# Interleaving the first two heads of differential attention with band attention, with outputs through DRAM and loads half a head ahead

## The chip, the core and the metric

The kernel runs on one core of a Trainium2 chip. The metric is the device time of one launch in microseconds (us). The core's engines are TensorE (PE in the profile; PEld is its weight load), VectorE (DVE), ScalarE (ACT) and GpSimd (POOL); SyncE (SP) issues nearly all DMA transfers of the stage that is changed.

## The reference, cut to what matters

One layer with 1024 rows of 1024 floats: a first feed-forward half step, two token mixers side by side, an output projection, a second feed-forward half step. The change touches the two mixers, A (band attention, 8 heads of 64) and B (differential attention, 4 heads, each with two score maps and values of 128).

```python
x = x + 0.5 * swiglu_ffn(rms_norm(x, ffn1_norm), ffn1_w_in, ffn1_w_out)
q_a, k_a, v_a, q_b, k_b, v_b, gate_logits = split(rms_norm(x, mix_norm) @ w_mix_in)
y_a = chunked_band_attention(q_a, k_a, v_a, rel_bias_a)         # own chunk of 64 and 8 before it
attn = softmax(s1 + bias) - lam * softmax(s2 + bias)            # B: chunk-causal, two maps
y_b = rms_norm(attn @ v_b, subln_g) * (1 - lambda_init)
g_a, g_b = split(sigmoid(gate_logits + b_gate))
x = x + (g_a * (y_a @ w_branch_a) + g_b * (y_b @ w_branch_b)) @ w_o
x = x + 0.5 * swiglu_ffn(rms_norm(x, ffn2_norm), ffn2_w_in, ffn2_w_out)
```

## The kernel before

**Stages.** The first feed-forward stage and the mixer's input projection come first; the projection writes queries, keys, values and gates to DRAM (`q_d`, `k_d`, `v_d`, `g_d`). The attention stage (pool `ps2`, from L747 on) reads them back head by head. The stage behind it (pool `ps3`) multiplies the outputs of B by `w_branch_b`, merges both branches and projects with `w_o`; the second feed-forward stage ends the kernel.

**Numbers as pairs.** A float that goes through a matmul as one operand is kept as a high and a low part (`split`, L94: a copy to the high part and a subtraction for the low part), so most products take two or three matmuls. The parts of queries share one tile `qs`, those of keys are two tiles `ks` and `kl`.

**Loads of a head.** `load_qkv` (L754 to L764) issues seven transfers on SP: `qs`, `ks`, `kl` in two halves of 512 KB each, and the values `vt` with 1024 KB. `bias_rows` (L794 to L803) fills the bias tile `nb`: two pieces of memory set by GpSimd and, for a pair of A heads, 8 transfers of 72 KB; for two B heads 4 of 128 KB and 4 of 120 KB. In A one load serves a pair of heads, so there are four loads, a0 to a3; B has four, b0 to b3, and one bias tile for two of them.

**Jobs.** A job is a Python generator whose pieces are laid out by `run` (L807): each new job is started, then each of the up to four jobs before it advances by one piece. In `jobs_a` (L815 to L874) a pair of heads is 8 jobs, each of two query blocks of 128 rows for one head: scores (L775, L776), softmax (L783, L785), scaling on GpSimd (L844), transposes (L791), the product with the values (L860), and at every second job the split of the sum into the output tile `y`. In `jobs_b` (L893 to L957) a head is 8 jobs, job i with one query block against i+1 key blocks, so the first is small and the last eight times as wide: two score maps, softmax, the difference, transposes, the product with the values (L939, L940), the norm, and a last matmul `try` (L954) that scales and transposes into `y`. All 32 jobs of A stand ahead of the 32 of B.

**The filler.** `branch_a` (L877 to L890) multiplies A's outputs with `w_branch_a` in 16 steps of 12 matmuls (tile `pb`), multiplies each result with its gate `gl`, which is loaded from DRAM in the step, and stores it as `ta`. In B, every second job calls one step (the sum `due`).

**Where a load comes in the order.** The first job of a head calls `load_qkv`, then takes an output tile, then the bias rows. All these tiles (`qs`, `ks`, `kl`, `vt`, `nb`, `y`, 8 KB in each of the 128 partitions) come from one pool of 14 buffers, `big` (L69). The outputs of all eight loads, `ys[0]` to `ys[7]`, keep their buffers until the filler and the next stage have used them, so fewer buffers are left for loads as the stage goes on.

**SP's queue.** SP issues its transfers in order. The build gives them eight semaphores in turn, so a transfer also waits until the eighth before it has landed. Temporary tiles of 2 KB (`gl`, sums, high parts) come from a pool `f` of 10 buffers. The order of instructions on each engine is fixed when the kernel is built.

Of the kernel before, what the change touches and what calls it, by code (L numbers as in the profile page):

```python
# [9 lines left out]
F32 = mybir.dt.float32  # L10
F32R = mybir.dt.float32r
# [5 lines left out]
P = 128  # L17
S = 1024
D = 1024
NT = S // P  # L20
# [24 lines left out]
RAW, WU, TF, TT = 10, 10, 10, 3  # L45
WA = 640
EA = 768
WB = 1024
HEADS = 5
SKEW = 32  # L50
EB = 1152
# [3 lines left out]
def hybrid_layer_kernel(ctx, tc, x, ffn1_norm, ffn1_w_in, ffn1_w_out, mix_norm, w_mix_in,  # L55
# [3 lines left out]
    nc = tc.nc  # L59
# [5 lines left out]
    sb = ctx.enter_context(tc.tile_pool(name="sb", bufs=1))  # L65
# [3 lines left out]
    def big(shape, name, dtype=F32R):  # L69
        return sb.tile(shape, dtype, tag="big", bufs=14, name=name)  # L70
# [51 lines left out]
    def move(eng, dst, src):  # L122

        eng.dma_start(out=dst.bitcast(F32), in_=src.bitcast(F32))
# [394 lines left out]
    def drams(n, shape, name, dtype=F32):  # L519
        return [dram.tile(shape, dtype, name=f"{name}{i}") for i in range(n)]  # L520
# [51 lines left out]
    ta_d = drams(KT, [P, S], "ta")  # L572
    diag_a = dram.tile([A_HEADS, SKEW, EA], F32, name="diag_a")
# [172 lines left out]
    ys = []  # L746
    with tc.tile_pool(name="ps2", bufs=1, space=PSUM) as ps:  # L747
# [59 lines left out]
        def run(jobs, filler=None):  # L807
            live = []
            for step, job in enumerate(list(jobs) + [None] * 4):
                for g in [job] + live[::-1] if job else live[::-1]:  # L810
                    next(g, None)
                live = (live + [job] if job else live)[-4:]


        def jobs_a(pr):  # L815
            ctx_ = {}

            def job(sb_, h):
                if not ctx_:
                    ctx_["qkv"] = load_qkv(pr)  # L820
                    ctx_["y"] = big([P, 2, S], "y")
                    ys.append(ctx_["y"])
                    ctx_["nb"] = big([P, 2, S], "nb", F32)
                    for hh in range(2):
                        bias_rows(ctx_["nb"][:, hh, :WA], diag_a, 2 * pr + hh, EA, WA)
                qkv, y, nb = (ctx_[n] for n in ("qkv", "y", "nb"))
# [44 lines left out]
                if h == 1:  # L871
                    c = slice(sb_ * 256, (sb_ + 1) * 256)
                    split(ysum, y[:, 0, c], y[:, 1, c], on_pool=True)
            return [job(sb_, h) for sb_ in range(4) for h in range(2)]  # L874


# [16 lines left out]
        def jobs_b(hb, filler):  # L893
            ctx_ = {}

            def job(i):
                if not ctx_:
                    ctx_["qkv"] = load_qkv(4 + hb)
                    ctx_["y"] = big([P, 2, S], "y")
                    ys.append(ctx_["y"])  # L900
                    if hb % 2 == 0:
                        nbs.append(big([P, 2, S], "nb", F32))
                        for hh in range(2):
                            bias_rows(nbs[-1][:, hh, :], diag_b, hb + hh, EB, WB)
                    ctx_["nb"] = nbs[-1][:, hb % 2, :]
                qkv, y, nb = (ctx_[n] for n in ("qkv", "y", "nb"))
# [45 lines left out]
                yield  # L952
                tr = ps.tile([P, 4, P], F32, tag="pt", bufs=2, name="try")
                nc.tensor.matmul(tr[:, 0, :], o1, dg, start=True, stop=True)  # L954
                c = slice(i * P, (i + 1) * P)
                split(tr[:, 0, :], y[:, 0, c], y[:, 1, c], scale=gsub)
            return [job(i) for i in range(NT)]  # L957

        jobs, nbs = [], []
        for pr in range(4):  # L960
            jobs += jobs_a(pr)
        filler = branch_a()
        due = [0]
        for hb in range(4):
            jobs += jobs_b(hb, filler)
        run(jobs)
        for _ in filler:
            pass
# [93 lines left out]
```

## Time and profile before

| what | value |
|---|---|
| time, median of 3 runs | 2185.04 us (2180.58 to 2188.15) |
| time of the profiled execution | 2184.25 us |
| its span in the profile | 2181.9 us |
| TensorE busy, share of the span | 2084.9 us, 96% |
| VectorE, ScalarE, GpSimd busy | 67%, 45%, 9% |
| bytes moved | 325.16 MB, 149 GB/s in the mean |
| granted TensorE clock, mean | 0.985 |
| attention stage | about 1076 to 1378 us of the span |

The profile is of one execution; its span leaves out 2.35 us of the measured time. A row of a windows view gives, for a stretch of the span, its length, then for each engine its busy time and number of instructions, the TensorE clock that was granted (1.00 is full speed), the busy share of the DMA engines and the rate. In a waits view a row names an instruction, what released it, the total of the time that its engine was idle ahead of it, how often, and the longest. In a timeline, the brackets at the end of a row hold the idle time just before it and its releaser.

### The profile page before, as it was taken

What the parts mean: (1) busy time and instruction counts of PE and PEld (TensorE: products, weight loads), DVE (VectorE), ACT (ScalarE), POOL (GpSimd) and SP (SyncE); (2) the same over time, 40 slices, a digit from 0 to 9 for tenths busy, and PEclk for the clock granted to TensorE, in tenths of its full rate; (3) what the DMA queues carried; (4) which work ended last, traced back from release to release, by engine and by line L of the source; (5) the groups of instructions that cost most, each with busy time, mean ns of one, the idle gap of its engine ahead of it and who ended that gap; (6) DMA issues with size and microseconds to landing.
All of it is one profiled execution on the core that took longest, in us unless ns stands there. A gap on an engine that the chain in (4) does not pass through costs nothing.

```text
span 2181.9 us, 29018 instructions
## 1 busy us (share of the span) xinstructions
PE 2084.9 (96%) x10025; PEld 1739.5 (80%) x10025; DVE 1461.3 (67%) x2678; ACT 977.4 (45%) x1911; POOL 195.6 (9%) x290
## 2 busy tenths in 40 slices
PE   6999999999999999999999878898999999999997
PEld 5788888888888788998788767676778888888886
DVE  7666565576578656556588767677766665658566
ACT  5433333334456444444588555235533333334444
POOL 2120000000000000000175233201000000000001
PEclk9999999999999999999999988999999999999999
DMA  6653233293354544443895675714543333366334
GB/s 191 175 167 113 91 107 102 91 373 105 116 167 128 164 136 164 135 151 125 210 210 122 156 180 157 243 64 145 173 130 120 96 114 97 116 221 233 98 116 158
DMA packets 273347, 325.16 MB, mean 149 GB/s; under 512 B 15292, under 2 KB 167884, under 8 KB 273200
## 3 DMA queue, kind: packets, MB, share of 16 engines
q1 hardware_dynamic: 271872, 319.55, 47.9%
q0 software_dynamic: 1184, 3.24, 0.6%
q8 instruction: 79, 1.29, 0.3%
q14 instruction: 68, 0.56, 0.1%
q10 hardware_dynamic: 144, 0.52, 0.1%
HBM read 226.45 MB, written 96.80 MB: 148 GB/s over the span
## 4 chain that ended last, share of the span: by engine, by line
PE 81%; DVE 7%; DMA 6%; ACT 3%; issue 2%; SPq 1%; POOL 0%; ACTq 0%; DVEq 0%; POOLq 0%
PE prod L128 18%; PE prod L129 18%; PE prod L130 18%; PE po L129 6%; PE po L130 6%; PE po L128 6%; DMA kl<-k 2%; DVE wlo L102 2%; PE tr L205 1%; ACT whi L97 1%; PE pt L791 1%; PE pb L128 1%; PE sc L775 1%; DMA ha<-hS 1%; PE pb L129 1%
## 5 line engine op out<-in xcount | busy, mean ns | idle before, releaser
L129 PE MATMUL po<-wlo,whi 128*128 128x512 f32 x728 | 284.7, 391 | 5.7 <-DVE wlo L102 5.5
L130 PE MATMUL po<-whi,wlo 128*128 128x512 f32 x728 | 283.4, 389 | 0.0
L97 ACT CAST whi<-raw 128x512 fp32r<-128x512 f32 x200 | 124.4, 622 | 308.6 <-PE prod L129 246.9
L97 ACT CAST whi<-T 128x512 fp32r<-128x512 f32 x196 | 121.9, 622 | 250.3 <-PE prod L129 225.1
L97 ACT CAST whi<-B 128x512 fp32r<-128x512 f32 x178 | 110.8, 623 | 266.0 <-PE po L129 258.0
L113 DVE TENSOR_TENSOR c<-prod,c 128x512 f32<-128x512 f32 x190 | 131.1, 690 | 134.6 <-PE prod L130 122.9
L102 DVE TENSOR_TENSOR wlo<-raw,whi 128x512 fp32r<-128x512 f32 x200 | 138.6, 693 | 105.1 <-ACT whi L97 66.4
L102 DVE TENSOR_TENSOR wlo<-B,whi 128x512 fp32r<-128x512 f32 x178 | 122.6, 689 | 126.7 <-ACT whi L97 126.6
L128 PE MATMUL po<-whi 128*128 128x512 f32 x728 | 198.4, 390 | 0.5 <-DVE xc L507 0.5
L102 DVE TENSOR_TENSOR wlo<-T,whi 128x512 fp32r<-128x512 f32 x196 | 134.7, 688 | 92.3 <-ACT whi L97 91.1
L139 POOL TENSOR_TENSOR r<-v,neg_half 128x1 f32<-128x1 f32 x64 | 53.8, 844 | 1326.8 <-DVE v L180 1227.1
L129 PEld LDWEIGHTS po<-wlo,whi 128*128 128x128 f32 x728 | 136.6, 188 | 37.7 <-DVE wlo L102 9.9
L128 PEld LDWEIGHTS po<-whi 128*128 128x128 f32 x728 | 136.2, 188 | 30.3 <-ACT whi L97 1.1
L130 PEld LDWEIGHTS po<-whi,wlo 128*128 128x128 f32 x728 | 136.7, 188 | 28.1
L102 DVE TENSOR_TENSOR wlo<-N,whi 128x512 fp32r<-128x512 f32 x64 | 44.1, 690 | 114.0 <-PE prod L129 62.8
L102 DVE TENSOR_TENSOR wlo<-ha,whi 128x512 fp32r<-128x512 f32 x154 | 105.7, 686 | 9.0 <-ACT whi L97 9.0
L272 ACT COPY c<-prod 128x512 f32<-128x512 f32 x186 | 103.1, 587 | 11.5 <-DMA hA<-c 4.0
L785 ACT ACTIVATE pm<-pm,mn 128x640 f32<-128x640 f32 (+7 forms) x128 | 94.1, 737 | 20.1 <-DVE mn L783 11.1
L783 DVE CUSTOM_DVE_ANT_0 pm<-sc,nb 128x640 f32<-128x640 f32 (+7 forms) x128 | 88.4, 699 | 21.5 <-PE sc L776 20.3
L97 ACT CAST whi<-ha 128x512 fp32r<-128x512 f32 x154 | 94.8, 615 | 16.9 <-PE prod L129 11.4
L128 PE MATMUL prod<-A11h,whi 128*128 128x512 f32 x240 | 96.0, 400 | 1.9 <-ACT A11h L97 1.9
L128 PE MATMUL prod<-S1h,whi 128*128 128x512 f32 x240 | 94.5, 394 | 2.4 <-ACT S1h L97 1.4
(246 smaller groups left out, 5398.3 us busy)
## 6 DMA issues: line engine op xcount, KB each, us to landing
raw<-in_ffn_w_in_dram SPq DMA_DIRECT2D x98, 512.0 KB, 4.4
raw<-in_w_mix_in_dram SPq DMA_DIRECT2D x47, 512.0 KB, 4.4
ha<-hS SPq DMA_DIRECT2D x88, 256.0 KB, 2.7
hA<-c SPq DMA_DIRECT2D x66, 256.0 KB, 4.3
ha<-hA SPq DMA_DIRECT2D x66, 256.0 KB, 2.7
B<-in_ffn_w_out_dram SPq DMA_DIRECT2D x12, 1024.0 KB, 10.6
hS<-hs SPq DMA_DIRECT2D x44, 256.0 KB, 2.8
hS<-c SPq DMA_DIRECT2D x44, 256.0 KB, 4.5
```

Of the source, the lines that this page charges most:

```text
L97: nc.scalar.copy(out=hi, in_=src)
L102: (nc.gpsimd if on_pool else nc.vector).tensor_tensor(out=lo, in0=src, in1=h, op=ALU.subtract)
L113: nc.vector.tensor_tensor(out=out_, in0=a, in1=b, op=op)
L128: nc.tensor.matmul(ps, a[0], b[0], start=first, stop=False, skip_group_check=shared)
L129: nc.tensor.matmul(ps, a[0], b[1], start=False, stop=False, skip_group_check=shared)
L130: nc.tensor.matmul(ps, a[1], b[0], start=False, stop=last, skip_group_check=shared)
L139: nc.gpsimd.tensor_tensor(out=r, in0=v, in1=neg_half, op=ALU.pow)
L205: nc.tensor.transpose(tr[:, k, :], rows[:, k * P:(k + 1) * P], ident)
L272: nc.scalar.copy(out=self.held[name], in_=p)
L775: nc.tensor.matmul(sc[:, m, :wc], qs[:, h, c], ks[:, h, kc], start=True, stop=False)
L783: nc.vector.tensor_tensor_reduce(out=d3, in0=sc, in1=nb.rearrange("p (n w) -> p n w", n=n), scale=1.0, scalar=3e38, op0=ALU.add, op1=ALU.m ...
L785: nc.scalar.activation(out=dst, in_=dst, func=AF.Exp, bias=mn, scale=-1.0, accum_out=rs)
```

## The change

- **Order of jobs.** The 16 jobs of b0 and b1 are put between the 32 jobs of A by the table `MIX` (a0.0 is job 0 of a0): b0.0 after the third A job, then one about every 2.7 A jobs; b1.0 comes after the 24th, and b1.3 to b1.7 behind the last. b2 and b3 follow as before.
- **Loads.** A head's loads are taken out of its first job into `begin()`, which now issues the bias rows ahead of `qs`, `ks`, `kl`, `vt`. The lists call `begin` early: a0 and b0 at the start, a1 before a0's fifth job, b1 before a1's first, a2 before a1's fifth, a3 before a2's fifth, b2 before a3's third, b3 after two jobs of b2.
- **Outputs.** An output is no longer kept in a `big` buffer: it is split into a small tile of pool `f` (`ya`, `yb`) and stored to `y_d` in DRAM: 16 stores of 256 KB for A, 24 of 128 KB for b0, b1 and b2. `load_y` reads them back, 1 MB each: `y0` to `y3` ahead of b2's first job, `y4` to `y6` ahead of b3's seventh. b3 writes its output tile directly.
- **Filler.** It is called only in b2 and b3, and there by every job: 16 steps in 16 jobs.
- **Pieces.** A job of B has one more `yield` ahead of `try`, and `run` keeps five jobs alive in place of four.

```diff
+MIX = [n * 12 // 32 for n in range(32)] + [16]
...
+    y_d = drams(7, [P, 2, S], "y", F32R)
...
+            for job in list(jobs) + [None] * 5:
+                if callable(job):
+                    job()
+                    continue
                 for g in [job] + live[::-1] if job else live[::-1]:
                     next(g, None)
-                live = (live + [job] if job else live)[-4:]
+                live = (live + [job] if job else live)[-5:]
...
+            def begin():
+                ctx_["nb"] = big([P, 2, S], "nb", F32)
+                for hh in range(2):
+                    bias_rows(ctx_["nb"][:, hh, :WA], diag_a, 2 * pr + hh, EA, WA)
+                ctx_["qkv"] = load_qkv(pr)
...
+                    y = sb.tile([P, 2, 256], F32R, tag="f", bufs=TF, name="ya")
+                    split(ysum, y[:, 0, :], y[:, 1, :], on_pool=True)
+                    move(nc.sync, y_d[pr][:, :, sb_ * 256:(sb_ + 1) * 256], y)
...
+        def load_y(n):
+            ys.append(big([P, 2, S], "y"))
+            move(nc.sync, ys[-1], y_d[n])
...
-                due[0] += 0.5
-                while due[0] >= 1:
-                    due[0] -= 1
+                if hb > 1:
                     next(filler, None)
...
                 yield
+                yield
                 tr = ps.tile([P, 4, P], F32, tag="pt", bufs=2, name="try")
...
+                    y = sb.tile([P, 2, P], F32R, tag="f", bufs=TF, name="yb")
+                split(tr[:, 0, :], y[:, 0, :], y[:, 1, :], scale=gsub)
+                if hb < 3:
+                    move(nc.sync, y_d[4 + hb][:, :, c], y)
...
+        loads = {(0, 0): (a[0], b[0]), (0, 4): (a[1],), (1, 0): (b[1],), (1, 4): (a[2],), (2, 4): (a[3],), (3, 2): (b[2],)}
+        jobs, mixed = [], b[0][1] + b[1][1]
         for pr in range(4):
+            for n, job in enumerate(a[pr][1]):
+                jobs += [l[0] for l in loads.get((pr, n), ())] + [job]
+                done = 8 * pr + n + 1
+                want = MIX[done]
+                while 16 - len(mixed) < want:
+                    jobs.append(mixed.pop(0))
+        jobs += [lambda n=n: load_y(n) for n in range(4)] + b[2][1][:2] + [b[3][0]] + b[2][1][2:]
+        jobs += b[3][1][:6] + [lambda n=n: load_y(n) for n in range(4, 7)] + b[3][1][6:]
```

**The start of the stage, on SP.** In the order before, a1's transfers stand right behind a0's, and a2's right behind those (`q1`, `q2` are the queries of a1 and a2, `v0` the values of A, `diag_a` the bias source of A):

```order
L124 DMA vt_9849<-v0_191 128x8x256
L801 DMA nb_9852<-diag_a_217 32x576 x8
L124 DMA qs_10315<-q2_177 64x2x1024
L124 DMA ks_10316<-k2_185 64x2x1024
L124 DMA kl_10317<-k2_185 64x2x1024
L124 DMA qs_10315<-q2_177 64x2x1024
L124 DMA ks_10316<-k2_185 64x2x1024
L124 DMA kl_10317<-k2_185 64x2x1024
L124 DMA vt_10324<-v0_191 128x8x256
L801 DMA nb_10327<-diag_a_217 32x576 x8
```

In the order after, this is what stands between a0's transfers and a1's: the bias rows of b0 and b1 (`diag_b`) and all of b0's transfers (`q4`, `k4`; `v1` holds the values of B), with gate stores of the projection (`g15`, `g7`) in between; a1's first bias rows are the last row:

```order
L804 DMA nb_9496<-diag_b_225 32x1024 x2
L126 DMA qs_9507<-q4_179 64x2x1024
L126 DMA ks_9508<-k4_187 64x2x1024
L126 DMA kl_9509<-k4_187 64x2x1024
L722 DMA g15_208<-c12_9399 128x512
L126 DMA qs_9507<-q4_179 64x2x1024
L126 DMA ks_9508<-k4_187 64x2x1024
L126 DMA kl_9509<-k4_187 64x2x1024
L722 DMA g15_208<-c22_9359 128x512
L126 DMA vt_9516<-v1_192 128x8x256
L804 DMA nb_9680<-diag_a_224 32x576 x4
```

What moved: b0's loads and B's bias rows went from behind a3 to a place ahead of a1.

**The same queue further on.** After a1's jobs have begun, a2's transfers now stand behind stores of output tiles (`y1` is a1's, `y4` is b0's):

```order
L126 DMA y4_221<-yb_10182 256x1x128
L126 DMA y1_218<-ya_10319 256x1x256
L126 DMA y4_221<-yb_10325 256x1x128
L804 DMA nb_10329<-diag_a_224 32x576 x8
L126 DMA qs_10342<-q2_177 64x2x1024
L126 DMA ks_10343<-k2_185 64x2x1024
L126 DMA kl_10344<-k2_185 64x2x1024
L126 DMA qs_10342<-q2_177 64x2x1024
L126 DMA ks_10343<-k2_185 64x2x1024
L126 DMA kl_10344<-k2_185 64x2x1024
```

What moved: a2's loads, which stood directly behind a1's, are now behind the y stores of a1's first jobs; of the buffers that they take, `nb`, `qs`, `ks` and `kl` are a1's `ks`, `qs`, `kl` and `nb`, where the order before had buffers that the stage ahead and a0 had left.

**TensorE at the third A job.** In the order before, this stood at the third job's product with the values (`pv`), between transposes (`pt`) and scores (`sc`) of a0 alone:

```order
L775 MATMUL sc_9667<-ks_9466,qs_9465 128x320
L776 MATMUL sc_9667<-kl_9467,qs_9465 128x320
L860 MATMUL pv_9697<-whi_9633,vt_9474 128x256
L775 MATMUL sc_9709<-ks_9466,qs_9465 128x320
L776 MATMUL sc_9709<-kl_9467,qs_9465 128x320
L775 MATMUL sc_9709<-ks_9466,qs_9465 128x320
L776 MATMUL sc_9709<-kl_9467,qs_9465 128x320
L791 MATMUL pt_9680<-ident_66,pm_9567 128x128
L791 MATMUL pt_9680<-ident_66,pm_9578 128x128
L791 MATMUL pt_9680<-ident_66,pm_9567 128x128
L791 MATMUL pt_9680<-ident_66,pm_9578 128x128
```

In the order after, the same product has b0's first scores in it (`ks_9508`, `kl_9509` and `qs_9507` are b0's tiles, `vt_9494` is a0's):

```order
L865 MATMUL pv_9736<-whi_9657,vt_9494 128x256
L778 MATMUL sc_9592<-ks_9508,qs_9507 128x128
L778 MATMUL sc_9600<-ks_9508,qs_9507 128x128
L865 MATMUL pv_9736<-wlo_9658,vt_9494 128x256
L865 MATMUL pv_9736<-whi_9657,vt_9494 128x256
L865 MATMUL pv_9736<-wlo_9658,vt_9494 128x256
L865 MATMUL pv_9736<-whi_9665,vt_9494 128x256
L865 MATMUL pv_9736<-wlo_9666,vt_9494 128x256
L865 MATMUL pv_9736<-whi_9665,vt_9494 128x128
L865 MATMUL pv_9736<-wlo_9666,vt_9494 128x128
L779 MATMUL sc_9592<-kl_9509,qs_9507 128x128
L779 MATMUL sc_9600<-kl_9509,qs_9507 128x128
```

What moved: b0's first four score matmuls went from behind a3's last jobs to the third job of a0, ahead of the scores of a0's fourth job.

More of the change, by code (lines that the diff above doesn't have):

```diff
@@ L803, in bias_rows, with run @@
                                               [[length - 1, SKEW], [1, c1 - c0]]))
-        def run(jobs, filler=None):
+        def run(jobs):
             live = []
-            for step, job in enumerate(list(jobs) + [None] * 4):
+            for job in list(jobs) + [None] * 5:
+                if callable(job):
+                    job()
+                    continue
                 for g in [job] + live[::-1] if job else live[::-1]:
                     next(g, None)
-                live = (live + [job] if job else live)[-4:]
+                live = (live + [job] if job else live)[-5:]
         def jobs_a(pr):
             ctx_ = {}
-            def job(sb_, h):
[L819 to L826, printed above, removed]
+            def begin():
[3 more added lines that the diff above has]
+                ctx_["qkv"] = load_qkv(pr)
+            def job(sb_, h):
+                qkv, nb = (ctx_[n] for n in ("qkv", "nb"))
                 vt = qkv[3]
@@ L894, in jobs_b, with begin @@
             ctx_ = {}
-            def job(i):
[L897 to L906, printed above, removed]
+            def begin():
+                if hb % 2 == 0:
+                    nbs.append(big([P, 2, S], "nb", F32))
+                    for hh in range(2):
+                        bias_rows(nbs[-1][:, hh, :], diag_b, hb + hh, EB, WB)
+                ctx_["nb"] = nbs[-1][:, hb % 2, :]
+                ctx_["qkv"] = load_qkv(4 + hb)
+            def job(i):
+                qkv, nb = (ctx_[n] for n in ("qkv", "nb"))
                 vt = qkv[3]
```

24 lines of the change are left out of this document (12 added, 12 removed).

## The prediction

> **What bounds the kernel now.** I read the page first. TensorE is busy 96% of the span at nearly full clock; the only tenths of its clock row below 9 lie past the middle, where the attention stage ends.
>
> ```profile
> span 2181.9 us, 29018 instructions
> ...
> PE 2084.9 (96%) x10025; PEld 1739.5 (80%) x10025; DVE 1461.3 (67%) x2678; ACT 977.4 (45%) x1911; POOL 195.6 (9%) x290
> ...
> PEclk9999999999999999999999988999999999999999
> ```
>
> So the question is where TensorE stands still in that stage. A windows view cuts it at the heads (columns: length, PE busy, PEld, DVE, ACT, POOL, granted clock, DMA share, GB/s). The first row is band attention, the next seven are b0's middle to b3's middle, in turn a head's work and the boundary to the next.
>
> ```profile
> 1075.80:1192.00 116.20, 107.29 (x750) 93.76 (x751) 100.59 (x324) 101.89 (x264) 74.04 (x93) 1.00 0.83 186
> 1192.00:1203.00 11.00, 10.62 (x63) 9.35 (x62) 10.64 (x30) 8.20 (x22) 4.33 (x7) 1.00 0.32 102
> 1203.00:1222.00 19.00, 10.98 (x59) 9.40 (x59) 10.25 (x32) 8.25 (x22) 4.19 (x8) 0.87 1.04 228
> 1222.00:1249.00 27.00, 26.41 (x156) 23.31 (x156) 23.02 (x75) 16.00 (x45) 7.37 (x16) 0.96 0.26 83
> 1249.00:1267.00 18.00, 10.91 (x68) 9.36 (x66) 11.80 (x33) 9.16 (x22) 7.38 (x12) 0.85 1.05 232
> 1267.00:1294.00 27.00, 26.76 (x154) 23.87 (x153) 20.25 (x71) 16.80 (x49) 8.09 (x17) 0.91 0.45 126
> 1294.00:1317.00 23.00, 13.24 (x70) 11.73 (x69) 11.94 (x34) 10.24 (x27) 4.08 (x7) 0.76 0.99 228
> 1075.00:1100.00 25.00, 22.04 (x152) 19.02 (x153) 20.33 (x67) 22.74 (x56) 17.41 (x22) 1.00 1.00 239
> ```
>
> Three boundaries (1203, 1249, 1294) have a DMA share of 1.0 and a half-idle TensorE: 19.0 − 11.0 = 8.0, 18.0 − 10.9 = 7.1 and 23.0 − 13.2 = 9.8 us, together 24.9. Between them the DMA engines have little to do (0.26 to 0.45). The waits view of TensorE over b0 to b3 names the cause, and the timeline shows b1's case.
>
> ```profile
> PE sc L775 <- DMA ks<-k: 16.9, 3, 8.0
> ```
>
> ```profile
> 1199.20 0.59 SPq L124 DMA_DIRECT2D qs<-q  x1
> ...
> 1205.65 0.40 PE L776 MATMUL sc<-kl,qs 128*128 128x512 f32 x1
> ...
> 1220.12 0.66 PE L776 MATMUL sc<-kl,qs 128*128 128x128 f32 x2 [0.21 <-DMA kl<-k]
> ```
>
> b1's load is issued at 1199.2, b0's last score runs at 1205.7, and b1's last keys are there at 1220.1: 20.9 us for a head's queries and keys, of which b0's remaining work covers a half.
>
> **What the change takes away.** b1 is loaded during A, b3 after two jobs of b2 (the six left, some 45 us with their fillers, against 17.9 us of load, worked out below), b2 during a3. The three waits go: −24.9. Their rows also show the clock at 0.87, 0.85 and 0.76. Applied to the whole stretches that would be 0.13 × 19 + 0.15 × 18 + 0.24 × 23 = 10.7 us, but part of it falls on idle time, and a wait that is only hidden costs no clock; I take 7 (0 to 10.7). Term: **−32**. The Trainium skill ("TensorE: Matmul & The Clock Gate", Part 1) says that the clock halves after an idle window of some 3.4 us; the three rows agree, with their 0.76 to 0.87.
>
> **What it adds at the start.** Sizes come from the DMA issues (KB each, median us to landing), moments from the timeline, rates from the last windows row above: at full share 0.228 to 0.239 MB per us; I take 0.235.
>
> ```profile
> qs<-q SPq DMA_DIRECT2D x16, 512.0 KB, 8.7
> ...
> vt<-v SPq DMA_DIRECT2D x8, 1024.0 KB, 18.5
> ...
> nb<-diag_a SPq DMA_DIRECT2D x32, 72.0 KB, 9.9
> ...
> nb<-diag_b SPq DMA_DIRECT2D x8, 128.0 KB, 9.4
> ...
> nb<-diag_b SPq DMA_DIRECT2D x8, 120.0 KB, 12.1
> ```
>
> ```profile
> 1049.21 0.67 SPq L124 DMA_DIRECT2D qs<-q  x1
> ...
> 1077.59 0.56 SPq L719 DMA_DIRECT2D g<-sig  x1
> ...
> 1085.26 0.28 PE L860 MATMUL pv<-whi,vt 128*128 128x256 f32 x1
> ...
> 1097.40 0.40 PE L775 MATMUL sc<-ks,qs 128*128 128x128 f32 x2
> ```
>
> A head is 6 × 512 KB + 1024 KB = 4.19 MB, 17.9 us; A's bias rows are 8 × 72 KB = 0.59 MB; B's, for two heads, 1.02 MB; a gate store of the projection, such as the one at 1077.6, is 256 KB, 0.26 MB. Before, the loads begin at 1049.2, a0's third job reaches its product with the values at 1085.3 and a1's first score comes at 1097.4, with no wait in any of them.
>
> *First wait, b0.* Behind the third A job's first `pv` now stand b0's first scores, and behind them all the rest of TensorE's order. Ahead of b0's keys in SP's queue are a0 with its bias (4.78), 8 gate stores (2.10), B's bias rows (1.02) and b0's own queries and keys (3.15): 11.05 MB, 47.0 us. From 1049.2 with 2 us of start-up that is 1098, against 1085.3: some **+12**, with 6 and 18 as bounds (a rate of 0.27, as if the gate stores went beside; a start 6 us later).
>
> *Second wait, a1.* b0's values, two more gate stores, a1's bias and its queries and keys are 1.05 + 0.52 + 0.59 + 3.15 = 5.31 MB: 22.6 us more, 1120.6. It is due at 1097.4 + 12 + the matmuls of b0's three small jobs that come before it: 24, at 117 us / 750 = 0.156 us each from the first windows row, 3.7 us; so at 1113. **+7.5** (0 to 12).
>
> *Third and fourth, a2 and a3.* Before, a2's and a3's loads take buffers that stand free. Now four of a2's five tiles take those of a1, so the load can only begin with a1's last score, and SP, which waits there in order, holds back the y stores behind it. GpSimd's memory set of a2's bias stands in the same way ahead of the scaling of A's next jobs. Eight bias transfers come first now, at their median issue time in the first of these rows (line L801; ns, min/median/max); the others are two transfers that stand around b1's load:
>
> ```profile
> L801 SPq DMA_DIRECT2D nb<-diag_a x32: 302/410/7687, 1063.1 to 1149.3; - x32
> ```
>
> ```profile
> 1198.71 0.39 SPq L119 DMA_DIRECT2D wa<-in_w_branch_a_dram  x1
> ...
> 1199.88 0.54 SPq L119 DMA_DIRECT2D gl<-g  x1
> ```
>
> 8 × 0.41 = 3.3 us. b1's 20.9 had a weight load and a gate load (512 and 256 KB, 3.3 us) in it, so a2's queries and keys take 17.6, with the bias 20.9. Between a1's last score and a2's first with `kl` stand 95 matmuls in TensorE's order, 14.8 us: **+6** (0 to 10). For a3, whose bias, queries and high keys take b0's tiles and whose low keys a2's, the same load (22 with a store ahead) stands against 104 matmuls from b0's last score, 16.2 us: **+6** (0 to 10).
>
> These four are 31.5. Their clock costs what it did at the boundaries: with 7 us per 24.9 of waiting it would be 9, but two of the four are short, so **+4** (0 to 10.8).
>
> **What it adds later.** The filler's 16 steps move into b2 and b3.
>
> ```profile
> 1192.00:1376.00 184.00, 46.30 (x180) 34.14 (x180) 10.69 (x16) 0.90 0.62 163
> ```
>
> ```profile
> DVE gl L888 <- DMA gl<-g: 9.2, 5, 3.3
> ```
>
> ```profile
> PE pb L128 <- DVE gl L888: 2.7, 1, 2.7
> ```
>
> ```profile
> gl<-g SPq DMA_DIRECT2D x32, 256.0 KB, 4.3
> ...
> ta<-gl SPq DMA_DIRECT2D x16, 256.0 KB, 2.4
> ```
>
> The rows are from windows of the tile `pb` alone, the waits of VectorE and TensorE, and the DMA issues; the first has 15 steps of 12 matmuls, 46.3 us, 3.1 a step; that work stays. But its gates (16 × 0.26), results (4.2) and weights (2.1), seven y tiles (7.3) and b3's load (4.2) make 22 MB in the last two heads, 94 us at 0.235, against about 50 us a head (40 as before, 12 for four more steps). So a gate load queues more often than now, when five of them held VectorE for 9.2 us and TensorE for 2.7: **+4**, from 0 to 16 (one us a step). The y stores themselves (7.3 MB) ride in A and b0/b1, whose DMA share outside the new waits is below 0.85, and nothing on TensorE waits for them; the first filler step needs `y0` to `y3` (4.2 MB, 17.9 us), whose buffers a3 and b1 leave; b1's last, wide jobs cover them, and if they didn't, a wait like the 10 of a boundary now would stand there, which the upper bound holds.
>
> **What it saves beside.** Two small terms from these rows:
>
> ```profile
> PE try L954 <- POOL dg L951: 3.9, 3, 2.2
> ...
> PE pv L939 <- ACT o L944: 2.3, 3, 0.9
> ```
>
> `try` comes a piece later: −2 (−3.9 to 0). Band attention leaves TensorE idle for 116.2 − 107.3 = 8.9 us, with ScalarE at 101.9 of 116.2; B's jobs ask less of ScalarE and may fill it, but a fifth live job also takes turns at two `sc` and two `pv` buffers: −2 (−9 to +4).
>
> **Sum.** −32 + 31.5 + 4 + 4 − 2 − 2 = +3.5 on the profiled execution's 2184.25 (its span 2181.9 and 2.35 beside it), which is 0.8 below the median of 2185.04: **2188**. 0.3%, 6.5 us, is about what a measurement of this kernel can tell from no change (its runs spread over 7.6). With the four waits each moved by a third of their bounds, 2176 to 2200.
>
> **Rivals.**
>
> *The loads fit (faster).* If the mixed work covers a1, a2 and a3 (b0's jobs lie between A's and lengthen what stands ahead of each score, and 0.156 us a matmul is too short where the clock is down), only b0's wait is left: 2188 − 19.5 − 3 of clock = **2165**. For it speaks that before, A ran through four loads without a wait at a share of 0.83; against it that these loads had free buffers and stood 20 to 60 us ahead. In the extreme the loads come so much faster that b0's wait goes too: −32 + 4 − 2 − 2 gives **2152**. The rows of 228 to 239 GB/s at full share speak against that. The Trainium skill ("HBM Reference", Specifications) has about 358 GB/s for a core; by that, an estimate, the 11.05 MB take 31 us and no wait is left; the three full-share rows here differ from it by a third.
>
> *The gate loads bind the last two heads (slower).* Every step waits as the five did, 9.2 / 5 = 1.84 us, 29 over 16 steps; TensorE felt 2.7 of 9.2 then, and would feel up to all of it where a step comes with every job. Halfway, 19 in place of 4: **2203**. It decides once 22 MB take longer than the two heads' work; 94 against some 104 us is near. For it: the share of 0.99 to 1.04 whenever a load runs; against it: a gate load is issued ahead of its product.
>
> *The change doesn't do it for b3 (slower).* Four y loads, the first gate load and weights stand ahead of b3's load on SP, and b3's tiles take b1's buffers. If the load lands as late as before, its 9.8 us stay: **2198**.
>
> **Chances.** The trade comes out even, 2188: 0.45 (0.10 of it faster, 0.25 the same, 0.10 slower by over 0.3%). The loads fit: 0.27, of it 0.22 for 2165 (0.01 of that the same) and 0.05 for 2152. Gate loads bind: 0.18. b3's wait stays: 0.10. Faster 0.10 + 0.21 + 0.05 = 0.36, same 0.26, slower 0.10 + 0.18 + 0.10 = 0.38. For 8 in 10 the range holds the even case, most of the 2165 case and of both slower ones: 2160 to 2208; it leaves out the 2152 case and the tails of its two neighbours.
>
> **What would show it.** In the changed kernel's waits view, `sc` for DMA of keys should have about four entries, the longest some 12 us at about 1086, and the windows at b1's, b2's and b3's first scores should be free of idle time. No entry there over 3 us in A means the loads fit. A total of VectorE's `gl` waits over 20 us in the last 100 us of the stage, and `pb` waiting for them, means the gate loads bind. A `sc` wait of 7 us or more at b3's first score means that its load is late. I am wrong as to kind if A's mixed part runs slower without any wait for DMA, by buffers of `sc`, `pv` or `f`.

## The result and the profile after

The changed kernel takes 2211.86 us (median of 4 runs, 2208.8 to 2215.11) against 2185.03 for the kernel before: the ratio is 1.0125, with a 95% interval of 1.0101 to 1.0148. It is slower by 26.8 us, above the range of 2160 to 2208.

First the page of the changed kernel: span, busy times, granted clock.

```profile
span 2208.5 us, 29125 instructions
...
PE 2091.0 (95%) x10025; PEld 1743.2 (79%) x10025; DVE 1466.5 (66%) x2678; ACT 977.2 (44%) x1911; POOL 193.2 (9%) x290
...
PEclk9999999999999999999899999899999999999999
```

The same 10025 matmuls take 6.1 us longer, and the clock row now has an 8 at the start of the attention stage as well as near its end. The loss is in that stage: its last matmul `try` ends at 1402.8 in place of 1376.8. A windows view from the first scores to that end (length, PE busy, PEld, DVE, ACT, POOL, granted clock, DMA share, GB/s), the whole stage of the kernel before:

```profile
1075.80:1377.90 302.10, 256.53 (x1601) 224.96 (x1601) 230.40 (x720) 201.76 (x529) 130.38 (x193) 0.94 0.70 172
```

and the changed kernel, whole and then cut at its waits:

```profile
1075.80:1404.00 328.20, 263.40 (x1604) 229.61 (x1602) 235.36 (x720) 203.01 (x530) 127.58 (x187) 0.91 0.76 205
...
1085.80:1097.30 11.50, 0.05 (x2) 0.06 (x1) 0.86 (x2) 0.27 (x1) 0.69 (x1) 0.65 1.04 221
1097.30:1118.00 20.70, 18.74 (x96) 15.68 (x96) 15.66 (x55) 14.35 (x40) 11.07 (x12) 0.78 0.99 233
1118.00:1123.20 5.20, 0.53 (x3) 0.38 (x2) 1.56 (x7) 1.51 (x5) 2.79 (x3) 0.68 1.03 238
1123.20:1166.00 42.80, 38.28 (x260) 34.25 (x260) 37.68 (x118) 35.07 (x91) 23.00 (x33) 0.96 0.84 199
1166.00:1173.00 7.00, 0.00 (x0) 0.00 (x0) 1.41 (x3) 1.29 (x4) 0.72 (x1) 0.86 1.04 206
1173.00:1208.90 35.90, 32.47 (x217) 29.71 (x217) 30.38 (x94) 28.27 (x73) 19.30 (x29) 0.93 0.47 118
1208.90:1215.70 6.80, 0.00 (x0) 0.03 (x1) 2.60 (x5) 1.19 (x4) 2.78 (x5) 0.73 1.06 241
1215.70:1300.00 84.30, 78.13 (x523) 69.05 (x523) 72.51 (x229) 64.10 (x171) 35.47 (x50) 0.98 0.77 201
1300.00:1306.00 6.00, 0.00 (x0) 0.00 (x0) 0.74 (x2) 0.00 (x0) 0.00 (x0) 0.85 0.81 244
```

The stage is 26.1 us longer: 6.9 of it are matmuls that run slower (263.4 − 256.5, with 1604 and 1601 of them recorded), 19.2 are idle time (64.8 − 45.6). There are five stretches in which TensorE does nothing, and a lower clock in or behind most of them. The waits view of TensorE over this stage names them:

```profile
PE sc L778 <- DMA ks<-k: 21.4, 3, 11.5
PE pv L946 <- DVE gl L898: 7.8, 3, 6.0
PE sc L778 <- DVE mn L786: 7.5, 17, 1.5
PE sc L778 <- issue: 7.0, 1, 7.0
...
PE sc L779 <- DMA kl<-k: 2.5, 3, 1.6
```

Rows of `sc` for keys come to 21.4 + 2.5 and the 7.0 at a2 that the view puts down to issue (the last of the keys' transfers was landing): 30.9 us, against 16.9 + 3.0 before. The timeline gives their places, and the prediction had all of them:

```profile
1097.27 0.66 PE L778 MATMUL sc<-ks,qs 128*128 128x128 f32 x2 [11.45 <-DMA ks<-k]
...
1121.10 0.45 PE L778 MATMUL sc<-ks,qs 128*128 128x128 f32 x1 [3.07 <-DMA ks<-k]
...
1123.14 0.44 PE L779 MATMUL sc<-kl,qs 128*128 128x128 f32 x1 [1.60 <-DMA kl<-k]
...
1173.04 0.77 PE L778 MATMUL sc<-ks,qs 128*128 128x128 f32 x2 [7.04 <-issue]
...
1215.70 0.45 PE L778 MATMUL sc<-ks,qs 128*128 128x128 f32 x1 [6.83 <-DMA ks<-k]
...
1306.01 0.58 PE L946 MATMUL pv<-vt,whi 128*128 128x256 f32 x1 [6.03 <-DVE gl L898]
```

b0's keys land at 1097.3 (worked out: 1098), a1's at 1121 to 1123 (1120.6); the waits are 11.5, 4.7, 7.0 and 6.8, 30.0 in all, where the sum had 12, 7.5, 6 and 6. At b1's, b2's and b3's first scores nothing waits for a load any more. The last row is new: 6 us at a product of B with its values. It takes turns at two buffers with the filler's `pb` and waits until VectorE has multiplied the filler's first result with its gate, so it waits for the gate's load. On SP's timeline around it, the gate stands behind the end of b3's load and behind a store of `yb` that took 7.1 us to issue:

```profile
1284.67 0.59 SPq L126 DMA_DIRECT2D vt<-v  x1
1286.10 7.09 SPq L126 DMA_DIRECT2D y<-yb  x1
1293.29 0.55 SPq L121 DMA_DIRECT2D gl<-g  x1
```

### The profile page after: what moved, and what is told of

Its sections match the earlier page's. It is cut to its first block, busy times and chain, and to the rows that moved or that the text cites. A ratio compares the mean times of both kernels' runs of the same rounds, so it can differ in the third digit from the quotient of the medians.

```text
span 2208.5 us, 29125 instructions
## 1 busy us (share of the span) xinstructions
PE 2091.0 (95%) x10025; PEld 1743.2 (79%) x10025; DVE 1466.5 (66%) x2678; ACT 977.2 (44%) x1911; POOL 193.2 (9%) x290
## 4 chain that ended last, share of the span: by engine, by line
PE 78%; DVE 9%; DMA 7%; ACT 3%; issue 2%; SPq 0%; ACTq 0%; DVEq 0%
PE prod L130 18%; PE prod L131 18%; PE prod L132 18%; PE po L131 6%; PE po L132 6%; PE po L130 6%; DVE wlo L104 3%; DMA kl<-k 1%; DMA vt<-v 1%; DVE pm L786 1%; DMA gl<-g 1%; PE tr L207 1%; ACT whi L99 1%; PE pb L130 1%; DVE B L115 1%
## 5 line engine op out<-in xcount | busy, mean ns | idle before, releaser
L778 PE MATMUL sc<-ks,qs 128*128 128x320 f32 (+5 forms) x192 | 71.1, 377 | 37.0 <-DMA ks<-k 21.4
L99 ACT CAST whi<-ha 128x512 fp32r<-128x512 f32 x154 | 94.8, 615 | 16.9 <-PE prod L131 11.4
```

Of the source, the lines that this page charges most:

```text
L99: nc.scalar.copy(out=hi, in_=src)
L778: nc.tensor.matmul(sc[:, m, :wc], qs[:, h, c], ks[:, h, kc], start=True, stop=False)
```

## The experiments

The theory after this look: **the kernel before has little room on the DMA engines in band attention and much in B; the change moves the loads of B to where there is none, takes the free buffers away with them, and pays for each wait a second time by the clock.** The rivals: mixing itself costs on TensorE; the outputs through DRAM and the crowded filler cost; the place of b0's scores alone is at fault. Times are medians beside a median of 2184.7 to 2186.4 for the kernel before on the same chip.

**b0 later.** `MIX` alone is shifted.

```diff
-MIX = [n * 12 // 32 for n in range(32)] + [16]
+MIX = [max(0, n - 6) * 12 // 26 for n in range(32)] + [16]
```

> Only the table MIX is changed: b0's first job comes after the ninth A job in place of the third; loads stay in their order. Theory one (the queue): a1's keys land about 1120 whatever TensorE does, since b0's load is ahead of them, so b0's wait of 11.5 us at 1097 goes and a1's, now 3.1 and 1.6 us, grows to 15 to 20: the time stays within 5 us of the changed kernel's 2212. Rival (the place of b0's scores in TensorE's order): b0's wait goes and nothing takes its place: 2195 to 2199, 11.5 us of waiting and some 4 of low clock behind it.

2218.3 us (ratio 1.0154, 1.0132 to 1.0176). The time is 6.5 us above the changed kernel's, 1.5 more than theory one allowed. b0's wait went and a1's took its place, larger than the two together (16.1):

```profile
1120.99 0.77 PE L778 MATMUL sc<-ks,qs 128*128 128x128 f32 x2 [19.75 <-DMA ks<-k]
```

a1's keys land at 1121 with b0's scores early or late. It is the queue, not the place of b0's scores.

**a1 before b0.** The queue's order is changed, and b0's jobs begin later.

```diff
-        loads = {(0, 0): (a[0], b[0]), (0, 4): (a[1],), (1, 0): (b[1],), ...
+        loads = {(0, 0): (a[0], a[1]), (0, 4): (b[0],), (1, 0): (b[1],), ...
+MIX = [max(0, n - 12) * 12 // 20 for n in range(32)] + [16]
```

> a1 is loaded right behind a0 and b0 half a head later; b0's first job comes after the fourteenth A job. Theory one (the queue): the waits of b0 and a1 (11.5 + 4.7 us) go, and with them the low clock behind them (0.78 over 20.7 us, 4.5 us); a2's and a3's waits of some 7 us each stay: about 2191, 2186 to 2196. Rival (buffers): b0's or b1's load now waits for a0's buffers and a wait as long comes at b0's first score: 2205 to 2212.

2219.6 us (1.0159, 1.0141 to 1.0177). A miss for both. a1 still waits 6.3 us at 1098, b0 4.2 at 1122, and a2 now 19.6 at 1165: a2's first bias transfer begins only at 1140.2, behind b1's load and stores of `ya` on SP, 9 us after a1's last score:

```profile
1164.58 0.77 PE L778 MATMUL sc<-ks,qs 128*128 128x128 f32 x2 [19.64 <-DMA ks<-k]
```

**b1 last.** As that, with b1 loaded ahead of a3's first job and a2 and a3 half a head sooner; b1's jobs follow A, and b2's load goes to b1's third job.

```diff
+        loads = {(0, 0): (a[0], a[1]), (0, 4): (b[0],), (1, 0): (a[2],), (2, 0): (a[3],), (3, 0): (b[1],)}
```

> As the kernel with a1 before b0, and b1 is loaded only ahead of a3's first job, so that a2 and a3 take free buffers early; b1's jobs all follow band attention. Theory one (a2 and a3 wait because b1 holds four buffers for sixteen A jobs): the two waits of 7.0 and 6.8 us and some 4 us of low clock go as well: about 2173, 2167 to 2180. Rival (mixing itself costs, by scores and products that take turns at two buffers each): the waits go but the time stays above 2185.

2196.0 us (1.0049, 1.0030 to 1.0069), 23.5 better than the one before it, and still short of the figure. a3's and b1's waits are gone, a1 and b0 wait about as in the run before (7.8 and 4.0 us), and a2, loaded early and put early by the build (its first score a few matmuls behind a1's last), waits 12.4 + 3.3 us at 1145 to 1150. Its keys land sooner than in the changed kernel (1173), but its scores were moved up further than its load.

**b1 moved alone.** The changed kernel with b0 first and mixed in as it is, and only b1 moved out of the way (b2's load, which stood ahead of a3's third job, goes to b1's third).

```diff
+        loads = {(0, 0): (a[0], b[0]), (0, 4): (a[1],), (1, 0): (a[2],), (2, 0): (a[3],), (3, 0): (b[1],)}
+MIX = [min(8, n * 12 // 32) for n in range(32)] + [16]
```

> The changed kernel with b1 moved alone: loaded ahead of a3, its jobs all behind band attention, so that a2 and a3 find free buffers and load half a head earlier; b0 stays mixed in and first in the queue. Theory one (a2 and a3 wait because a load can only begin with the last score of a1 and of b0): their waits of 7.0 and 6.8 us go, b0's and a1's of 11.5 and 4.7 stay: 2192 to 2200. Rival (the DMA engines have no room in that stretch, so that an earlier start does not land earlier): a2 still waits 5 us or more, 2203 to 2212.

2194.0 us (1.0039, 1.0025 to 1.0053), 17.8 less than the changed kernel. a2 and a3 don't wait; b0's and a1's waits are as before:

```profile
PE sc L778 <- DMA ks<-k: 15.6, 2, 12.8
...
PE sc L779 <- DMA kl<-k: 2.0, 1, 2.0
```

So a2's and a3's 13.9 us go when b1's four tiles, loaded some 90 us before use, are not taken and the two loads are asked for sooner. The traces point to the buffers: in the changed kernel a1's last score starts at 1152.1 (L779) and a2's first bias transfer at 1152.7; here that transfer starts at 1112.8, before a1's first score. The run changes both things at once, so how much the sooner call gives alone is not shown.

**No mixing.** All of A, then B; early loads, outputs through DRAM and the filler as in the changed kernel.

```diff
-MIX = [n * 12 // 32 for n in range(32)] + [16]
+MIX = [0] * 33
+        loads = {(0, 0): (a[0],), (0, 4): (a[1],), (1, 4): (a[2],), (2, 4): (a[3],), (3, 4): (b[0],)}
+        jobs += b[0][1][:2] + [b[1][0]] + b[0][1][2:] + b[1][1][:2] + [b[2][0]] + b[1][1][2:]
```

> All 32 A jobs first, then b0 to b3, as in the order before; loads half a head ahead, outputs through DRAM and the filler in the last two heads as in the changed kernel. Theory one (the early loads are good and the interleaving of b0 and b1 makes the new waits): no wait for keys at any head; what is left against the kernel before is minus 20 of waiting, minus some 7 of low clock, plus 8 to 10 for the gates' waits in the last two heads: 2167, 2160 to 2176. Rival (outputs through DRAM and the crowded filler cost by themselves as much as the boundary waits did): 2180 to 2192.

2187.1 us (1.0008, 0.9993 to 1.0023): no difference from the kernel before can be told, which is the rival's number. The mixing costs 24.8 us of the 26.8, but the early loads with outputs through DRAM gain nothing either: TensorE's idle time in the stage is as long as before (45.3 and 45.6 us), and its matmuls take 4.9 us longer. The trace shows two waits that come in place of the old ones. a1 waits 6.7 us (5.1 + 1.6, to 1098), though b0 isn't ahead of it: the build, told of a load half a head early, puts a1's first score 100 matmuls behind a0's first, where the order before had 129. And at 1221 VectorE waits for a small buffer of pool `f` that a `ya` store still holds, since the store was queued on SP behind b0's bias rows and load; TensorE stands 7.7 us for it:

```profile
1221.05 0.29 DVE L955 CUSTOM_DVE_ANT_0 sq<-o 128x128 f32<-128x128 f32 x1 [6.93 <-DMA y<-ya]
```

**B alone.** The kernel before, in which A keeps its order, its loads and its outputs on chip; only b0's, b1's and b2's outputs go through DRAM, and the buffers so won hold the next head's load after two jobs.

```diff
-                if not ctx_:
-                    ctx_["qkv"] = load_qkv(4 + hb)
-                    ctx_["y"] = big([P, 2, S], "y")
+            def begin():
+                ctx_["qkv"] = load_qkv(4 + hb)
...
+                if hb < 3:
+                    move(nc.sync, y_d[hb][:, :, c], y)
...
+        for hb in range(3):
+            jobs += b[hb][1][:2] + [b[hb + 1][0]] + b[hb][1][2:]
+        jobs += b[3][1][:6] + [lambda n=n: load_y(n) for n in range(3)] + b[3][1][6:]
```

> Band attention exactly as before (its order, its loads, its outputs kept on chip, the window of four, the filler at every second B job); only B is changed: b1, b2 and b3 are loaded after two jobs of the head before, into the buffers that are free because b0's, b1's and b2's outputs go to DRAM by tiles and come back in b3. Theory one (the stretch of A has no room on the DMA engines, the stretch of B has): the three waits at b1, b2 and b3, 19.9 us for keys and some 7 of low clock, go and no new wait of over 3 us comes: 2158 to 2166. Rival (the outputs through DRAM cost: their stores stand in SP's queue behind a head's load and hold the small buffers): 2172 to 2182.

2172.8 us (0.9944, 0.9930 to 0.9958), faster than both kernels, at the fast end of the rival's range and above theory one's. No wait for keys is left, in A or B; the rival holds in part, since TensorE now waits for the gates for 11.6 us:

```profile
PE pv L946 <- DVE gl L896: 10.0, 3, 6.9
...
PE pb L128 <- DVE gl L896: 1.6, 1, 1.6
```

**b3 later.** One number of the changed kernel: `b[2][1][:4] + [b[3][0]]` in place of `[:2]`.

> One number of the changed kernel: b3 is loaded after four jobs of b2 in place of two. Theory one (the first gate load of the filler stands behind b3's load in SP's queue, so TensorE waits 6.0 us at 1306): that wait goes, b3's load is still there in time: 2203 to 2207. Rival (the four outputs of A, read back, are what the first step waits for): no change, 2209 to 2215.

2209.5 us (1.0114, 1.0099 to 1.0129), within the noise of the changed kernel, as the rival had it. But this told nothing of the cause: the order that the build made still has b3's load ahead of the gate (queries at 1281.7, gate at 1294.6), and the wait is there, 6.3 us.

**Gates early.** The filler loads each gate two steps ahead; its first two are asked for four jobs before the end of b1.

```diff
+            gates = [gate(0), gate(1)]
+            yield
...
-                        gl = load(g_d[j][:, c], temp([P, HALF], "gl"))
+                        gl = gates.pop(0)
+                        if 2 * j + n < 14:
+                            gates.append(gate(2 * j + n + 2))
```

> The changed kernel with each gate of the filler loaded two steps ahead, the first two ahead of b3's load on SP. Theory one (the wait of 6.0 us at 1306 is the first gate behind b3's load; the later gate waits, 3.6 us, are the crowd in the last two heads): the first goes and about half of the rest: 2203 to 2207. Rival (the wait is for the read-back of A's outputs, which take the same DMA engines): 2209 to 2214.

2198.6 us (1.0062, 1.0049 to 1.0075), 13.3 less, more than either expected. Gate waits fall from 9.6 to 1.1 us; but in the first one's place stands another, for ScalarE, which waited 6.8 us for a small buffer that a `yb` store held:

```profile
1309.49 0.58 PE L951 MATMUL pv<-vt,whi 128*128 128x256 f32 x1 [5.21 <-ACT o L956]
```

The stage is 4.2 us shorter by its profile (324.0 of 328.2), the last product with `w_branch_b` (1452.3 for 1457.9) 5.6 earlier. Behind that, where no instruction differs, the profiled run takes 745.9 us in place of 750.6. Six other profiles, of the kernels before and after and of four experiments, have 749.7 to 752.2 us there. Those 4.7 us are not explained by the edit, so no more than about 6 us of the 13.3 can be put down to the gates.

The same edit on the kernel that changes B alone:

> The kernel that changes B alone, with only the gates of the filler loaded two steps ahead. If the gates' waits are a matter of when they are asked for: 2162 to 2167, and the added piece and fifth job are worth the difference from the run with both. Rival (DMA engines busy): 2170 to 2175.

2168.5 us (0.9925, 0.9912 to 0.9938): between the two. A wait of 4.8 us for ScalarE stays near the place where 6.9 had been waited for the gate. With the added piece and the window of five as well:

> The kernel that changes B alone (2172.8), with the gates of the filler loaded two steps ahead and with the changed kernel's added piece and window of five. If the gates' waits there (10.0 and 1.6 us in TensorE's waits) are a matter of when the gate is asked for, and the waits of the last matmul for GpSimd (3.7 us) of the added piece: 2160 to 2165. Rival (the gates wait for the DMA engines, busy with a head's load, whenever they are asked for): 2170 to 2175.

2168.0 us (0.9924, 0.9912 to 0.9936), the same, and again between the two. These two are the fastest kernels of the study, some 17 us under the kernel before; which of the two can't be told.

**The old window.** The changed kernel with four live jobs and without the added `yield`.

```diff
-                live = (live + [job] if job else live)[-5:]
+                live = (live + [job] if job else live)[-4:]
...
-                yield
                 yield
                 tr = ps.tile([P, 4, P], F32, tag="pt", bufs=2, name="try")
```

> The changed kernel with the window of four jobs and without the added yield ahead of the last matmul of a B job. If the two together save what the prediction took (2 us by the later matmul, and 2 by mixing): 2214 to 2218. Rival (a fifth live job takes turns at two score and two product buffers and costs): 2203 to 2209.

2223.7 us (1.0179, 1.0161 to 1.0197): the two are worth 11.8 us in the mixed order, three times what was taken, though none in the order of B alone. `try` waits for GpSimd there, which scales A's tiles in between:

```profile
PE try L961 <- POOL dg L958: 14.1, 6, 3.9
```

**Idle matmuls.** To part the clock from the waiting, matmuls that nothing reads are put where TensorE waits.

```diff
+        def keep_warm(n):
+            t = ps.tile([P, HALF], F32, tag="pt", bufs=2, name="warm")
+            for _ in range(n):
+                nc.tensor.matmul(t[:, :P], ident, ident, start=True, stop=True)
```

> The changed kernel with idle matmuls put ahead of the first scores of b0 (44), a2 (26) and a3 (26); they add to nothing that is read, and lie where TensorE waits for keys. Theory (the waits cost a second time, by the clock that is granted behind them: 0.78 over 20.7 us, 0.93 over 35.9, 0.96 over 42.8): the waits look shorter, the clock row stays near 1.0 and the time falls by 5 to 9, to 2203 to 2207. Rival (the low clock is hidden by the waits for keys that come next): no change within 3 us, or slower by what dummies stand outside of a wait.

2221.2 us (1.0164, 1.0149 to 1.0180). It failed as a test: the build put the idle matmuls of a2 and a3 behind the waits that they were to fill, and those of b0 end 7.7 us before its keys are there. The four waits stay at 9.5, 3.6, 8.2 and 7.2 us, 28.5 in all where the changed kernel has 30.0, while the added matmuls take 22.5.

**Both, and b0 late.** b1 moved and gates early together; then b0's load also put off to a1's fifth job, its first job after the 22nd.

> The changed kernel with b1 moved and the gates loaded early, both. If the two are separate costs they add: 2212 - 17.8 - 13.3 = 2181, 2178 to 2185, and b0's and a1's waits of some 12 and 5 us are still there. Rival (one shared crowd of transfers, moved about): 2188 to 2195, no better than the better one by more than 6.

2194.6 us (1.0035, 1.0019 to 1.0051): they don't add. With b1 moved the gates had already lost most of their wait (3.4 of 9.6 us left), so the second edit had only that to save, and a wait of 5.6 us for the small buffers came with it.

> As the kernel with both, and b0 loaded only ahead of a1's fifth job, its first job after the 22nd A job. Theory (b0 at the head of the queue costs its wait, a1's, and the low clock behind them, 16 + 5 us): b0's wait goes, a1's of some 7 stays as in the run without mixing: about 2170, 2165 to 2175. Rival (the transfers of b0 only move on and a wait as long comes at b0's or a3's first score): 2178 to 2186.

2193.4 us (1.0034, 1.0021 to 1.0048): the rival's mechanism, at more than its price. b0's wait at 1097 is gone, and the same time is waited at a1 (6.2), b0 (4.8) and a3 (5.1 + 6.2), 22.3 in all where the run with both had 18.3:

```profile
1151.48 0.45 PE L779 MATMUL sc<-kl,qs 128*128 128x128 f32 x1 [4.82 <-DMA kl<-k]
...
1168.87 0.44 PE L778 MATMUL sc<-ks,qs 128*128 128x128 f32 x1 [5.06 <-DMA ks<-k]
...
1175.53 0.44 PE L779 MATMUL sc<-kl,qs 128*128 128x128 f32 x1 [6.21 <-DMA kl<-k]
```

**Extra transfers.** The kernel before with loads that nothing reads, ahead of a1's, then ahead of a1's, a2's and a3's.

```diff
+                    if pr == 1:
+                        for d in (q_d[0], k_d[0]):
+                            move(nc.sync, big([P, 2, S], "extra"), d.rearrange("c p s -> p c s"))
                     ctx_["qkv"] = load_qkv(pr)
```

> The kernel before with two loads of 1 MB into tiles that nothing reads, ahead of a1's load: 2.1 MB, 8.9 us at 0.235 MB per us. Theory (band attention's stretch is full: a DMA share of 0.92 to 1.03 there): the loads behind them land that much later, a wait of 5 to 9 us comes at a1's or a2's first score and some 3 of low clock: 2191 to 2198. Rival (there is room): 2185 to 2188, no wait for keys of over 2 us in band attention.

> The same ahead of a1, a2 and a3: 6.3 MB, 26.7 us of the DMA engines, about what the outputs of A and b0's load add to that stretch in the changed kernel. Theory (full): 15 to 27 us of waits in band attention and some 5 of clock: 2203 to 2216. Rival (room): 2185 to 2192.

2189.7 us (1.0022, 1.0012 to 1.0032) and 2195.4 us (1.0048, 1.0031 to 1.0065): 4.3 us for 2.1 MB and 10 for 6.3 MB, 1.6 to 2 us per MB. That is under the 4.25 of a full queue and well over nothing: both expectations missed, and "full" is too strong. The build counts the added transfers too and puts a1's first score 172 matmuls behind a0's, so the keys are there in time; what is left in A shows as 4.2 and 4.9 us ahead of a score at 1110, behind VectorE's wait for a1's bias rows (2.9 and 3.6 us), and as a low clock, in the first of the two runs:

```profile
1075.80:1125.00 49.20, 42.57 (x270) 37.66 (x270) 37.19 (x121) 39.05 (x99) 28.67 (x40) 0.90 0.99 232
```

In this stretch 270 matmuls run where the kernel before had 307 at a clock of 1.00. Over that run's whole stage the idle time is no longer than before (45.0 and 45.6 us); all of the loss is matmul time (262.2 and 256.5). The added tiles also take buffers of `big`, which the two runs don't part from their bytes.

## Why the prediction was wrong

The forecast was +3.5 us on the profiled execution; the stage came out at +26.1. By the prediction's own terms:

- **The new waits** (+31.5): right in place, cause and size, 30.0 measured. The bytes ahead of b0's and a1's keys divided by 0.235 MB per us gave their landing within 3 us; that a2's load begins with a1's last score is in the trace. "b0 later" shows the queue; "b1 moved" agrees with the buffers, but moved b1's transfers as well.
- **The waits that go** (−24.9): too large by 5.0. They went, but they were 16.9 + 3.0 = 19.9 us of waiting for keys; the other 5.0 in my windows was idle time of other causes, which a load in time doesn't remove. The waits row that I quoted had the smaller number; I took the window's.
- **The clock** (−7 for the old waits, +4 for the new): this step failed most, by 9.9 us (−3 against +6.9 of matmul time in the stage). Cut into half microseconds, the granted clock of the stage is 1.00 or 0.50, with few windows between. Behind b0's wait it is 0.50 for 8.8 us and then 1.00 until a1's wait:

```profile
1097.30:1106.00 8.70, 8.10 (x28) 6.76 (x29) 4.81 (x20) 3.78 (x13) 1.96 (x2) 0.50 1.00 273
1106.50:1118.00 11.50, 10.14 (x68) 8.42 (x66) 10.85 (x35) 10.07 (x28) 9.11 (x10) 1.00 1.02 211
```

  If a matmul takes twice as long at 0.50, half of TensorE's busy time at 0.50 is what the low clock costs. That is an estimate: scores of 320 columns follow each other at 0.27 us before 1106 and at 0.15 behind it. The busy time at 0.50 is 21.2 us behind the three old waits and 20.4 behind the four new ones, so the old ones cost 10.6 us and the new ones 10.2, where I had 7 and 4: the trade of waits gains almost nothing by the clock. I had priced the removed idle time at 7 / 24.9 = 0.28 us per us and the added at 4 / 31.5 = 0.13, on the ground that two waits were short; but the cost doesn't follow the length: 2.0 us behind a1's 4.7, 1.6 behind a3's 6.8, 4.2 behind b0's 11.5.

  The rest is where the sum had no term for it: 2.2 us behind the new wait for the gate, and low stretches behind shorter pauses, most of them in the stage's last 45 us. Over the whole stage TensorE is busy at 0.50 for 40.8 us against 28.2 before; half of the difference is 6.3 of the 6.9. The estimate holds over the runs: TensorE's busy time in the stage goes from 253.1 to 272.1 us in the seventeen kernels without idle matmuls, and with half of the time at 0.50 taken off it is 241 to 246 in all of them. The run that should have parted the clock from the waiting failed, so this is a reading of traces.

  The Trainium skill ("TensorE: Matmul & The Clock Gate", Part 1) has the clock halved by an idle window of about 3.4 us and full again after a busy one as long. The trace agrees in kind: in the changed kernel's five waits the clock falls 1.9 to 5.2 us after TensorE stops, and it is back 3.4 to 4.9 us after TensorE starts again, 8.8 behind b0's wait.
- **The filler's gates** (+4, 0 to 16): right in kind, 6.9 us more of gate waits (9.6 against 2.7), 6.0 of them in one place, the first step behind b3's load. I had looked for the y loads there. "Gates early" shows that asking sooner removes the gate's wait and leaves one for the small buffers.
- **What it saves beside** (−4): not seen. All other idle time is 1.3 us more than before. The added piece and the fifth job do save 11.8 us, but only what the mixed order costs without them; scores that wait for a free buffer rose from 3.2 to 7.5 us.

Misses of 4.4 (keys, 5.0 less the 0.6 by which the waits view has the new ones smaller), 2.9, 5.3 and 9.9 us make 22.5 of the 22.6 between forecast and profile. Of the rivals, "gate loads bind" came nearest in sign, but not in mechanism: it had all sixteen steps wait, 19 us; TensorE waited 6.9 us more than before, 6.0 of it in one step, and VectorE's gate waits in the last 100 us of the stage are 16.2, under the 20 that I had set as its sign. The range failed because its upper end came from one rival at a time, with every wait at the size in the sum and the clock taken as nearly free.

What stays open: the 4.7 us that "gates early" gained behind the stage, and how to be rid of the wait of some 5 us that comes back each time the gates are asked for sooner. The traces name what holds the small buffer then, a store of `yb` or `ta` (ScalarE waits 3.9 to 6.8 us for it in the five runs); no run removes it.

## What to carry to other kernels

Before a transfer is moved earlier, look at the DMA share of the stretch that it is moved into and at whose buffers it takes: here the share was 0.99 in the first 50 us of band attention, and every mixed order waited 16 us or more for keys, at a place that moved with the order. Fetching ahead paid where the room was, in B, with A left alone: 13.6 us, and some 17 with the gates asked for sooner. And a wait is priced with the clock behind it, by the same rule for those that go and those that come: here 1.6 to 4.2 us for each, short or long.

## What the runs showed of the hardware

- What the DMA engines move at full share depends on the transfers. The loads of heads moved 221 GB/s between 1085.8 and 1097.3 in the changed kernel and 232 in the first 49 us with extra transfers, both at a share of 0.99 or more; the two rows of the changed kernel's page, share in tenths and GB/s in 40 slices, have 358 at a share of 0.9 or more in the ninth slice. The Trainium skill ("HBM Reference", Specifications) has about 358 GB/s per core: a slice reaches that figure here, the loads of heads nowhere in the stretches above, so the rate to work with was that of the same transfers. Three loads of outputs, `y`, go faster than either, as the last row below shows for a stretch of the changed kernel; my 0.235 MB per us was too low for them. Queries and keys fill 64 partitions, 512 KB each, a `y` tile 128 and 1024 KB; no run parts these two differences.

```profile
DMA  6653233393344544443986866734543333357334
GB/s 191 174 161 120 91 110 96 104 358 101 115 158 148 166 134 155 154 144 117 241 200 154 225 174 207 253 111 133 153 148 119 96 119 96 111 206 246 96 115 158
...
1252.00:1260.00 8.00, 7.34 (x53) 6.61 (x51) 7.38 (x19) 7.22 (x18) 4.27 (x5) 1.00 1.04 422
```

- A wait on SP for a transfer's turn holds everything behind it: `y<-yb` took 7.1 us to issue behind b3's load, and the gate behind it was used 12 us after it was issued.
